# Written program order for three engines and the output weights' sums in a fused attention and SwiGLU layer

## The chip, the cores and the metric

The kernel runs on one core of a Trainium2 chip. The time is that of one execution of the whole program on the device, in microseconds (us); lower is better. A profile is one execution taken apart by the hardware profiler.

## What is computed

One layer (DEPTH = 1) with SEQ = 1024 rows, D_MODEL = 1024 and D_FF = 2816 in float32: attention with forget gates, then a SwiGLU feed-forward layer, each added to its input under a gate and normalised. The rest of the reference (the other mixer) isn't reached with one layer. What matters here is the second half of the loop body:

```python
def swiglu(h, w_in, w_out):
    gate, up = jnp.split(h @ w_in, 2, axis=-1)
    return (jax.nn.silu(gate) * up) @ w_out
...
        x = layer_norm(DEEPNORM_ALPHA * x + gate1 * y, ln_g[i, 0], ln_b[i, 0])
        h = x * (1.0 + scale2) + shift2
        x = layer_norm(DEEPNORM_ALPHA * x + gate2 * swiglu(h, ffn_w_in[i], ffn_w_out[i]), ln_g[i, 1], ln_b[i, 1])
```

## The kernel before

Each float32 operand is split into a high and a low part; a product takes three matmuls on TensorE (PE): high by high, high by low, low by high.

**The first feed-forward product** (h by the input weights) is where the change lies. It goes by hidden blocks of 128 columns, ff = 0 to 21, and multiplies 2 by 2 blocks with seven products in place of eight, called i = 1 to 7. Operand i of the weights is a part of the two weight tiles of the block (wi, gate half and up half) or a sum of such parts; operand i of h is a tile X or a part of h. The list `seq` holds the steps (ff, i): for the first six blocks products 1 and 2 alone are done first (12 steps, n = 0 to 11); then each of these blocks takes five steps (6, 7, 5, 4, 3), and each later block seven (1, 6, 2, 7, 5, 4, 3), 154 steps in all. `step(n)` does in this order:

- an eleventh of the output weights' sums, `out_weights(j, k)`, if one is due at this step (from step 42, ten steps for each j): loads of two weight tiles on the queue of SyncE (SP) at k = 0, two VectorE (DVE) subtractions at k = 7 (L1008, L1009), two more at k = 8 (L1011, L1012) and two stores of the result, the DRAM tile td, also on SP;
- the step's 12 matmuls (L1072 to L1074), which add into a PSUM bank: A for i = 1, 2; B for 6, 7, 4; D for 5, 3. Products of one bank accumulate, and between two of them the bank is read out;
- what is late: stores of hidden tiles, and for each pair of blocks four sums of hidden tiles, `hidden_sums`, on DVE (L990, L991, L994, L995);
- the read of the bank: i = 1 by a copy on ScalarE (ACT, L1081); i = 2 by ACT (L1083); i = 6 by DVE (L1085), which must be over before i = 7 adds into the same bank; i = 7 by DVE (L1087), before i = 4; i = 5 by DVE (L1089), before i = 3; i = 4 by DVE (L1092) and then GpSimd (POOL, L1093); i = 3 by DVE (L1096), ACT (L1097) and POOL (L1098);
- `prepare(n + 8)`: the weight operand of the step eight later goes into a ring of eight slots, the high part by ACT (L844), the low part by DVE (L845). At the first operand of a block, `sums(ff)` makes the sums: s1 for i = 5 (L828), s3 for i = 7 (L829), a21 in place for i = 6 (L830), s4 for i = 3 (L831), on DVE for ff < 2 and on POOL after that.

In the first steps the second half of the rows of h is still being made: `second_half(k)`, k = 0 to 3, and its later part `others`, transpose on PE, and make the five X tiles by ACT (L959, and L965 for the casts) and DVE (L960, L961, L966, L969, L970).

**The second product** (L1221 to L1223) follows, with a ring of its own: a cast by ACT (L1028) and a subtraction by DVE (L1029), and copies of PSUM by ACT (L1180).

**What sets the order.** The kernel is written as a sequence, but each engine's program is laid down by a scheduler, which moves an instruction ahead of others that it doesn't depend on, by its own estimate. Each engine then works its instructions off in that order.

Of the kernel before, what the change touches and what calls it, by code (L numbers as in the profile page):

```python
# [12 lines left out]
ALU = mybir.AluOpType  # L13
# [3 lines left out]
P = 128  # L17
# [22 lines left out]
def move(nc, dst, src):  # L40

    (nc.sync).dma_start(dst.bitcast(F32), src.bitcast(F32))


@with_exitstack
def fox_trunk_kernel(
# [17 lines left out]
    nc = tc.nc  # L64
# [5 lines left out]
    fwo = ffn_w_out[0]  # L70
# [230 lines left out]
    def qk_store(nm, ci, th):  # L301

        gi, dst = (0, qs) if nm[0] == "q" else (1, ks)
        g = gcol[:, gi:gi + 1]
        for p2 in range(2):
            st = bankS(f"st{nm}{th}{p2}")
            for i in range(4):
                qn = xh[nm, th * 4 + i].rearrange("p h d -> p (h d)")
                for k in range(2):
                    pr = p2 * 2 + k  # L310
                    nc.tensor.transpose(st[:, k, i * P:(i + 1) * P], qn[:, pr * P:(pr + 1) * P], ident)
            hi = pw.tile([P, 2, 512], F32R, name=f"qh{nm}{th}{p2}", tag="qth", bufs=1)
            lo = pw.tile([P, 2, 512], F32R, name=f"ql{nm}{th}{p2}", tag="qtl", bufs=1)
            nc.scalar.activation(hi, st, AF.Copy, scale=g)
            nc.vector.scalar_tensor_tensor(lo, st, g, f32(hi), op0=ALU.mult, op1=ALU.subtract)
            for k in range(2):
                d = dst[ci * 4 + p2 * 2 + k]
                for part, tl in ((0, hi), (1, lo)):
                    move(nc, d[part, :, th * 512:(th + 1) * 512], tl[:, k, :])

    def v_store(acc, tt, ci):
        vt = pv.tile([P, 4, 4, HD], F32R, name=f"vt{ci}{tt}", tag="vt", bufs=2)
        a4 = acc.rearrange("p (a b d) -> p a b d", b=2, d=HD)
        nc.scalar.copy(vt[:, :, 0::3, :], a4)
        nc.vector.tensor_tensor(vt[:, :, 1:3, :], a4, f32(vt[:, :, 0::3, :]), ALU.subtract)
        move(
            nc, vs[ci][:, tt * P:(tt + 1) * P, :].rearrange("h p e -> p h e"),
            vt.rearrange("p a b d -> p (a b d)").rearrange("p (h e) -> p h e", e=P),
        )

    def forget():
# [11 lines left out]
        def half(th):  # L343
# [40 lines left out]
            for r in range(2):  # L384
                move(nc, fq[:, r, cs], onesr)
                move(nc, fk[:, 2 + r, cs], onesr)
# [81 lines left out]
    def load(h):  # L468
        pr, s = divmod(h, 2)
        pool = ld[s]  # L470
        qa = pool.tile([P, T], F32R, name=f"qa{h}", tag="qa")
        ka = pool.tile([P, T], F32R, name=f"ka{h}", tag="ka")
        qb = pool.tile([68, T], F32R, name=f"qb{h}", tag="qb")
        kb = pool.tile([68, T], F32R, name=f"kb{h}", tag="kb")
        va = pool.tile([P, TT, P], F32R, name=f"va{h}", tag="va")
        rows = slice(s * HD, (s + 1) * HD)
        for r in range(2):
            move(nc, qa[r * HD:(r + 1) * HD, :], qs[pr][r, rows, :])
            move(nc, ka[r * HD:(r + 1) * HD, :], ks[pr][0, rows, :])
        move(nc, qb[0:HD, :], qs[pr][0, rows, :])  # L480
        move(nc, qb[HD:68, :], fq[h])
        move(nc, kb[0:HD, :], ks[pr][1, rows, :])
        move(nc, kb[HD:68, :], fk[h])
        move(nc, va, vs[h // 8][h % 8].rearrange("(k p) e -> p k e", p=P))
        return qa, qb, ka, kb, va
# [20 lines left out]
    first = load(0)  # L506
# [256 lines left out]
    def spill(tt):  # L763
        nc.sync.dma_start(x1d[tt], row(tt))
# [36 lines left out]
    def load_w(ff, n, tag):  # L801
        t = ld[0].tile([P, KT, P], F32, name=f"wi{ff}{n}_{len(opened)}", tag=tag, **({"bufs": 1} if tag == "owr" else {}))
        col = n * DFF + ff * P
        nc.sync.dma_start(t, fwi[:, col:col + P].rearrange("(k p) e -> p k e", p=P))
        opened.append(t)
        return t

    def load_raw(ff):
        raws[ff] = [load_w(ff, n, RAWS[ff % 2 * 2 + n]) for n in range(2)]
# [49 lines left out]
    td = [dram.tile([P, 2, 2, 512], F32, name=f"td{j}") for j in range(NJ)]  # L859
# [84 lines left out]
    def second_half(k):  # L944

        sp = bankS(f"h2t{k}")
        for n in range(2):
            for i in range(4):
                kt = n * 4 + k
                nc.tensor.transpose(sp[:, n, i * P:(i + 1) * P], row(HB * 4 + i)[:, kt * P:(kt + 1) * P], ident)  # L950
        a, a4 = [fp.tile([P, 512], F32, name=f"a{n}_{k}", tag=f"a{n}") for n in range(2)]
        for t, kt in ((a, k), (a4, k + 4)):
            nc.sync.dma_start(t, had[kt])
        hb = fp.tile([P, 512], F32, name=f"hb0_{k}", tag="hb0", bufs=2)
        ht = fp.tile([P, 2, 512], F32, name=f"ht_{k}", tag="hb1")
        hb4, t2 = ht[:, 0], ht[:, 1]
        for n, t in enumerate((hb, hb4)):
            kt = n * 4 + k
            nc.scalar.activation(t, sp[:, n, :], AF.Identity, scale=colA[:, kt:kt + 1], bias=colB[:, kt:kt + 1])  # L959
        nc.vector.tensor_tensor(a, hb, a, ALU.subtract)  # L960
        nc.vector.tensor_tensor(t2, hb4, a, ALU.subtract)  # L961

        def split(*parts):
            for n, t in parts:
                nc.scalar.copy(X[n][:, 0, k, :], t)  # L965
                nc.vector.tensor_tensor(X[n][:, 1, k, :], t, f32(X[n][:, 0, k, :]), ALU.subtract)  # L966

        def others():
            nc.vector.tensor_tensor(hb, hb4, hb, ALU.subtract)  # L969
            nc.vector.tensor_tensor(a4, a4, t2, ALU.subtract)  # L970
            split(("T3", hb), ("T4", a4), ("B22", hb4))
        split(("T2", t2), ("T1", a))
        return others

    banks, fds = {}, []

    def open_bank(tag, ff, n):
        banks[tag, ff] = psA.tile([P, 512], F32, name=f"{tag}{ff}", tag=tag, bufs=n)
# [21 lines left out]
    def out_weights(j, k):  # L1000

        b11, b12 = gate1b[:, 0:512], gate1b[:, 512:1024]
        b21, b22 = gate2b[:, 0:512], gate2b[:, 512:1024]
        if k == 0:
            for n, t in enumerate((gate1b, gate2b)):
                nc.sync.dma_start(t, fwo[(2 * j + n) * P:(2 * j + n + 1) * P, :])
        elif k == 7:
            nc.vector.tensor_tensor(b11, b12, b11, ALU.subtract)  # L1008
            nc.vector.tensor_tensor(b12, b22, b12, ALU.subtract)  # L1009
        elif k == 8:  # L1010
            nc.vector.tensor_tensor(b22, b22, b11, ALU.subtract)  # L1011
            nc.vector.tensor_tensor(b21, b21, b22, ALU.subtract)  # L1012
            for n, t in enumerate((gate1b, gate2b)):
                nc.sync.dma_start(td[j][:, n].rearrange("p c e -> p (c e)"), t)


    RING = 14
# [33 lines left out]
    def run_late(n):  # L1051

        for w in [w for w in late if w[0] <= n]:
            late.remove(w)
            w[1]()

    def step(n):
# [9 lines left out]
        if 0 <= j < NJ:  # L1067
            out_weights(j, k)
# [43 lines left out]
        prepare(n)  # L1112
    for ff in range(2):
        load_raw(ff)
    for n in range(n_first):
        step(n)
        if n in (3, 5, 7, 9):
            rest()
        if n in (2, 4, 6, 8):
            rest = second_half(n // 2 - 1)  # L1120
        if n == 8:
            for i in range(4):
                spill(HB * 4 + i)
    for n in range(n_first, len(seq)):
        step(n)
    run_late(len(seq) + 4)
    for cm in (fp_cm, psA_cm):
        cm.__exit__(None, None, None)
    fp = ctx.enter_context(tc.tile_pool(name="fo", bufs=1, side="right", reuse_waits="tile"))
# [173 lines left out]
```

## Time and profile before

| | |
|---|---|
| time, median of 3 runs | 1439.01 us (1437.71 to 1443.9) |
| profiled execution, its own time | 1438.14 us |
| its span, first to last instruction | 1436.3 us |
| mean granted clock of TensorE | 0.990 |
| busy: PE, DVE, ACT, POOL | 95%, 70%, 41%, 23% of the span |
| first feed-forward product | about 750 to 1211 us of the span |
| second product begins | about 1211 us |

Times in the rows are us from the start of the span. A timeline row has the start, the length, engine, line and operation; what stands in brackets is how long the engine had been idle and what ended that. The row of a window gives for each engine the busy time in it and, in brackets, its instructions.

### The profile page before, as it was taken

Reading aid. Unit: us, or ns where it says so; the run is one execution under the profiler, and the core shown is the slowest. Engines: PE = TensorE matmul, PEld = TensorE weight load, DVE = VectorE, ACT = ScalarE, POOL = GpSimd, SP = SyncE. Lnnn points to the kernel's source line nnn. Section 1 sums busy time; section 2 is a strip of 40 time slices with the busy share of each in tenths; the row PEclk is TensorE's granted clock in tenths of the full one; section 3 lists DMA queues with packets and bytes.
Section 4 is the critical chain, followed back from the end, with each engine's and each line's share of the span. In section 5 each row is a group of like instructions: output and inputs, shape, how many; then the busy total and the mean of one; then the engine's idle time right before and its main releaser. Section 6 shows DMA issues by size and latency. Waiting matters only on the chain.

```text
span 1436.3 us, 19137 instructions
## 1 busy us (share of the span) xinstructions
PE 1359.0 (95%) x6832; PEld 1134.0 (79%) x6832; DVE 1012.2 (70%) x1636; ACT 584.2 (41%) x1025; POOL 334.4 (23%) x250
## 2 busy tenths in 40 slices
PE   5899999999999999999999888999999999899997
PEld 4677778877888888879998667777788888788886
DVE  6866586555888888888778555767655556775897
ACT  3532232224777777774338222222223334533320
POOL 2442012210111111141000544434444431000011
PEclk9999999999999999999999999999999999999999
DMA  9757775558555555627463234777732336976531
GB/s 275 197 176 243 240 218 177 183 194 212 143 135 137 132 139 136 148 87 266 162 193 93 89 110 132 259 243 261 248 111 96 110 111 208 352 256 225 195 119 73
DMA packets 212305, 254.41 MB, mean 177 GB/s; under 512 B 13353, under 2 KB 138609, under 8 KB 212210
## 3 DMA queue, kind: packets, MB, share of 16 engines
q1 hardware_dynamic: 211058, 251.09, 57.9%
q10 hardware_dynamic: 1152, 2.10, 0.4%
q8 instruction: 54, 0.88, 0.3%
q14 instruction: 41, 0.34, 0.1%
HBM read 185.18 MB, written 67.96 MB: 176 GB/s over the span
## 4 chain that ended last, share of the span: by engine, by line
PE 63%; DVE 14%; DMA 9%; POOL 6%; issue 4%; ACT 2%; SPq 1%; POOLq 0%; DVEq 0%; ACTq 0%
PE og L631 5%; PE t L596 4%; PE y L1221 4%; PE y L1223 4%; PE y L1222 4%; PE B L1072 3%; PE B L1073 3%; PE B L1074 3%; PE s L535 2%; PE A L1072 2%; PE A L1074 2%; PE A L1073 2%; PE s L536 2%; PE o L579 2%; PE D L1074 2%
## 5 line engine op out<-in xcount | busy, mean ns | idle before, releaser
L1221 PE MATMUL y<-ring 128*128 128x512 f32 (+1 forms) x319 | 122.8, 385 | 4.7 <-ACT fpu L1180 4.3
L1072 PE MATMUL B<-XT,slots 128*128 128x512 f32 x264 | 106.9, 405 | 19.7 <-DVE fd L1085 16.7
L1029 DVE TENSOR_TENSOR ring<-r,ring 128x1024 fp32r<-128x1024 f32 x77 | 95.6, 1249 | 41.3 <-ACT ring L1028 36.2
L1028 ACT CAST ring<-r 128x1024 fp32r<-128x1024 f32 x77 | 80.5, 1053 | 107.7 <-PE y L1223 57.5
L1222 PE MATMUL y<-ring 128*128 128x512 f32 (+1 forms) x319 | 122.7, 385 | 0.0
L1223 PE MATMUL y<-ring 128*128 128x512 f32 (+1 forms) x319 | 122.4, 385 | 0.0
L602 DVE TENSOR_TENSOR pl<-t,ph 128x512 fp32r<-128x512 f32 x192 | 103.9, 549 | 14.8 <-ACT ph L601 13.4
L844 ACT CAST slots<-wi 128x512 fp32r<-128x512 f32 x88 | 54.2, 621 | 143.9 <-PE D L1073 73.0
L543 ACT ACTIVATE p<-s,nm 128x640 f32<-128x640 f32 (+7 forms) x128 | 95.5, 746 | 39.1 <-DVE nm L542 38.7
L601 ACT CAST ph<-t 128x512 fp32r<-128x512 f32 x192 | 90.9, 479 | 44.2 <-PE t L596 41.8
L1073 PE MATMUL B<-XT,slots 128*128 128x512 f32 x264 | 105.2, 399 | 0.0
L1074 PE MATMUL B<-XT,slots 128*128 128x512 f32 x264 | 105.0, 398 | 0.0
L542 DVE TENSOR_REDUCE nm<-s 128x1 f32<-128x640 f32 (+7 forms) x128 | 95.6, 748 | 2.5
L596 PE MATMUL t<-ident,p 128*128 128x128 f32 x576 | 95.7, 274 | 0.6 <-DVE pl L602 0.5
L596 PEld LDWEIGHTS t<-ident,p 128*128 128x128 f32 x576 | 71.3, 141 | 11.5 <-DVE pl L602 2.2
L1072 PEld LDWEIGHTS B<-XT,slots 128*128 128x128 f32 x264 | 50.9, 193 | 36.1 <-DVE fd L1085 21.8
L579 PE MATMUL o<-ph,va 128*128 128x512 f32 x192 | 76.6, 399 | 0.0
L845 DVE TENSOR_TENSOR slots<-wi,slots 128x512 fp32r<-128x512 f32 x88 | 71.0, 807 | 7.7 <-ACT slots L844 7.7
L1221 PEld LDWEIGHTS y<-ring 128*128 128x128 f32 x319 | 60.3, 189 | 18.1 <-ACT fpu L1180 4.7
L535 PE MATMUL s<-ka,qa 128*128 128x320 f32 (+2 forms) x192 | 67.5, 352 | 4.8 <-ACT p L543 4.8
L1223 PEld LDWEIGHTS y<-ring 128*128 128x128 f32 x319 | 60.4, 189 | 11.8
L1072 PE MATMUL A<-h2h,slots 128*128 128x512 f32 x176 | 69.2, 393 | 0.6 <-ACT fc L1081 0.6
(571 smaller groups left out, 3731.8 us busy)
## 6 DMA issues: line engine op xcount, KB each, us to landing
wi<-in_ffn_w_in_dram SPq DMA_DIRECT2D x50, 512.0 KB
aw<-in_ada_w_dram SPq DMA_DIRECT2D x46, 512.0 KB
r<-sd SPq DMA_DIRECT2D x77, 256.0 KB
sd<-hs SPq DMA_DIRECT2D x44, 256.0 KB
r<-td SPq DMA_DIRECT2D x44, 256.0 KB
sd<-fd SPq DMA_DIRECT2D x33, 256.0 KB
r<-in_ffn_w_out_dram SPq DMA_DIRECT2D x33, 256.0 KB
qa<-qs SPq DMA_DIRECT2D x32, 256.0 KB
```

The lines of the kernel that those rows point to most:

```text
L535: nc.tensor.matmul(o, qa[:, q], ka[:, c0:c0 + w], start=True, stop=False)
L542: nc.vector.tensor_reduce(nm, view, axis=axis, op=ALU.max, negate=True)
L579: nc.tensor.matmul(o[:, c0:], va[:, kbk, :], ph[:, c0:], start=(kbk == 0), stop=False)
L596: nc.tensor.transpose(tb[:, jj * P:(jj + 1) * P], probs[hf * 4 + jj][:, kbk * P:(kbk + 1) * P], ident)
L602: nc.vector.tensor_tensor(pl[:, c0:], tb[:, c0:], f32(ph[:, c0:]), ALU.subtract)
L1029: nc.vector.tensor_tensor(t[:, 1], raw, f32(t[:, 0]), ALU.subtract)
L1072: nc.tensor.matmul(b, hi, rh, start=(first and k == 0), stop=False, skip_group_check=True)
L1073: nc.tensor.matmul(b, hi, rl, start=False, stop=False, skip_group_check=True)
L1074: nc.tensor.matmul(b, lo, rh, start=False, stop=(k == 3), skip_group_check=True)
L1221: nc.tensor.matmul(b[:, c0:c1], sh, wh, start=first, stop=False, skip_group_check=True)
L1222: nc.tensor.matmul(b[:, c0:c1], sh, wl, start=False, stop=False, skip_group_check=True)
L1223: nc.tensor.matmul(b[:, c0:c1], sl, wh, start=False, stop=last, skip_group_check=True)
```

## The change

A new function, `written_order`, goes over the instructions in the order in which the kernel's text issued them and binds each one of ACT, DVE and POOL to the one before it on the same engine, with a dependence that the scheduler must keep but that puts no semaphore on the chip. It is called after the last step of the first product, for what was issued since the first step. PE and SP are not in its list. In `out_weights`, `tc.keep_in_program_order` is put around the loads, the four subtractions and the stores. No instruction is added or taken away.

```diff
+def written_order(tc, first, engines):
+
+    last = {}
+    for ins in tc.nc.cur_bb.bb.instructions[first:]:
+        if ins.engine not in engines:
+            continue
+        if ins.engine in last:
+            tc.add_manual_dep(ins, last[ins.engine],
+                              mybir.DependencyInfo(mybir.DependencyClass.NoSync, mybir.DependencyReason.DATA),
+                              reason="written order")
+        last[ins.engine] = ins.name
...
+    keep = tc.keep_in_program_order
...
         if k == 0:
             for n, t in enumerate((gate1b, gate2b)):
-                nc.sync.dma_start(t, fwo[(2 * j + n) * P:(2 * j + n + 1) * P, :])
+                keep(nc.sync.dma_start(t, fwo[(2 * j + n) * P:(2 * j + n + 1) * P, :]))
         elif k == 7:
-            nc.vector.tensor_tensor(b11, b12, b11, ALU.subtract)
-            nc.vector.tensor_tensor(b12, b22, b12, ALU.subtract)
+            keep(nc.vector.tensor_tensor(b11, b12, b11, ALU.subtract))
+            keep(nc.vector.tensor_tensor(b12, b22, b12, ALU.subtract))
         elif k == 8:
...
+    traced = len(nc.cur_bb.bb.instructions)
     for n in range(n_first):
         step(n)
...
     run_late(len(seq) + 4)
+    written_order(tc, traced, (mybir.EngineType.Activation, mybir.EngineType.DVE, mybir.EngineType.Pool))
```

The subtractions at k = 8 and the stores of td are wrapped in the same way. New lines shift the line numbers of the changed kernel: sums L828 to L831 become L841 to L844, L844 and L845 become L857 and L858, L990, L994, L995 become L1004, L1008, L1009, the output weights' L1008, L1009, L1011, L1012 become L1022, L1023, L1025, L1026, and the reads L1081, L1085, L1087, L1089, L1092, L1093, L1096, L1097, L1098 become L1095, L1099, L1101, L1103, L1106, L1107, L1110, L1111, L1112.

**GpSimd, the sums of block 14.** The wi140 and wi141 tiles are the gate and the up half of block 14. Before, from the row behind the last sum of block 13 on (the first L1093 and L1098 are those of block 11, the last two those of block 12):

```order
L1093 TENSOR_TENSOR fd_8631<-fd_8631,fc_8277 128x512
L1098 TENSOR_TENSOR fd_8631<-fd_8631 128x512
L829 TENSOR_TENSOR sqb_8409<-wi140_35_9958,wi141_36_9960 128x512
L828 TENSOR_TENSOR sqb_8409<-wi141_36_9960 128x512
L830 TENSOR_TENSOR wi141_36_9960<-sqb_8409,wi140_35_9958 128x512
L831 TENSOR_TENSOR skb_8410<-wi140_35_9958,wi141_36_9960 128x512
L1093 TENSOR_TENSOR fd_8631<-fd_8631,fc_8277 128x512
L1098 TENSOR_TENSOR fd_8631<-fd_8631 128x512
```

Of the change, from L1112 of block 12 on (L1107 and L1112 further down are those of block 13):

```order
L1112 TENSOR_TENSOR fd_8631<-fd_8631 128x512
L841 TENSOR_TENSOR sqb_8409<-wi141_36_9960 128x512
L842 TENSOR_TENSOR sqb_8409<-wi140_35_9958,wi141_36_9960 128x512
L843 TENSOR_TENSOR wi141_36_9960<-sqb_8409,wi140_35_9958 128x512
L844 TENSOR_TENSOR skb_8410<-wi140_35_9958,wi141_36_9960 128x512
L1107 TENSOR_TENSOR fd_8631<-fd_8631,fc_8277 128x512
L1112 TENSOR_TENSOR fd_8631<-fd_8631 128x512
L841 TENSOR_TENSOR sqb_8409<-wi151_38_10095 128x512
```

The four sums of a block now stand behind the last GpSimd operation of the block two before it, where they stood one block earlier, and L828 is now ahead of L829.

**VectorE, the first five-step blocks.** B1 is the bank of block 1, hs3_1 a hidden sum of blocks 0 and 1. Before:

```order
L1096 TENSOR_TENSOR fd_8631<-D0_8666,fd_8631 128x512
L845 TENSOR_TENSOR slots_7830<-sqb_8409,slots_7830 128x512
L994 TENSOR_TENSOR hs3_1_8840<-fd_8631 128x512
L1085 TENSOR_TENSOR fd_8631<-B1_8719,fc_8277 128x512
L845 TENSOR_TENSOR slots_7830<-wi21_12_8543,slots_7830 128x512
```

Of the change, at the same read of bank B1 (L1099 is L1085):

```order
L1106 TENSOR_TENSOR fd_8631<-B0_8630,fc_8277 128x512
L858 TENSOR_TENSOR slots_7830<-sqb_8409,slots_7830 128x512
L1110 TENSOR_TENSOR fd_8631<-D0_8666,fd_8631 128x512
L858 TENSOR_TENSOR slots_7830<-sqb_8409,slots_7830 128x512
L1099 TENSOR_TENSOR fd_8631<-B1_8719,fc_8277 128x512
L858 TENSOR_TENSOR slots_7830<-wi21_12_8543,slots_7830 128x512
L1101 TENSOR_TENSOR fd_8631<-B1_8719,fc_8277 128x512
L858 TENSOR_TENSOR slots_7830<-skb_8410,slots_7830 128x512
```

The hidden sum L994 stood ahead of the read of bank B; it is now behind it.

**VectorE, the second half of h, k = 1.** XT2_8272, XT1_8274, XT3_8273, XT4_8275 and XB22_8276 are the X tiles for i = 6, 5, 7, 4 and 3, hb0_1 and ht_1 what ACT makes of the transposes (L959). Before:

```order
L960 TENSOR_TENSOR a0_1_8426<-hb0_1_8430,a0_1_8426 128x512
L845 TENSOR_TENSOR slots_7830<-sqb_8409,slots_7830 128x512
L961 TENSOR_TENSOR ht_1_8431<-ht_1_8431,a0_1_8426 128x512
L966 TENSOR_TENSOR XT1_8274<-a0_1_8426,XT1_8274 128x512
L969 TENSOR_TENSOR hb0_1_8430<-ht_1_8431,hb0_1_8430 128x512
L966 TENSOR_TENSOR XT2_8272<-ht_1_8431,XT2_8272 128x512
L970 TENSOR_TENSOR a1_1_8427<-a1_1_8427,ht_1_8431 128x512
L966 TENSOR_TENSOR XT3_8273<-hb0_1_8430,XT3_8273 128x512
L966 TENSOR_TENSOR XB22_8276<-ht_1_8431,XB22_8276 128x512
L966 TENSOR_TENSOR XT4_8275<-a1_1_8427,XT4_8275 128x512
```

Of the change (L973, L974, L982, L983 and L979 are L960, L961, L969, L970 and L966):

```order
L973 TENSOR_TENSOR a0_1_8426<-hb0_1_8430,a0_1_8426 128x512
L974 TENSOR_TENSOR ht_1_8431<-ht_1_8431,a0_1_8426 128x512
L979 TENSOR_TENSOR XT2_8272<-ht_1_8431,XT2_8272 128x512
L979 TENSOR_TENSOR XT1_8274<-a0_1_8426,XT1_8274 128x512
L858 TENSOR_TENSOR slots_7830<-sqb_8409,slots_7830 128x512
L982 TENSOR_TENSOR hb0_1_8430<-ht_1_8431,hb0_1_8430 128x512
L983 TENSOR_TENSOR a1_1_8427<-a1_1_8427,ht_1_8431 128x512
L979 TENSOR_TENSOR XT3_8273<-hb0_1_8430,XT3_8273 128x512
L979 TENSOR_TENSOR XT4_8275<-a1_1_8427,XT4_8275 128x512
L979 TENSOR_TENSOR XB22_8276<-ht_1_8431,XB22_8276 128x512
L858 TENSOR_TENSOR slots_7830<-sqb_8409,slots_7830 128x512
```

The low parts now come in the order in which the text has them, T2 and T1 first, and no operation of `others` stands between L960 and the low part of T1 any more.

The subtractions of the output weights stand at their written steps in the changed program; in blocks 7 and 17 L1011 and L1012 (as L1025 and L1026), in block 14 L1008 and L1009, come between the low part of the next block's i = 6 (L845) and the read of bank B (L1085). On SP the loads and stores of the output weights, which all stood in the first half of the blocks, are now spread over the steps up to the last block, and the last store of td stands near the first loads of the second product's ring. In the second product ACT's first copies L1180 come after the cast of r2_18, where they came after that of r2_22.

## Rows read from the trace of the kernel before

**Rows 1.** The page, section 1: busy us, share of the span, instructions.
```profile
PE   1359.0 (95%) x6832; PEld 1134.0 (79%) x6832; DVE 1012.2 (70%) x1636; ACT 584.2 (41%) x1025; POOL 334.4 (23%) x250
```

**Rows 2.** Stretches: window, its us, busy per engine (instructions), granted clock, DMA share, GB/s.
```profile
800.00:900.00 100.00, 87.79 (x355) 70.42 (x354) 52.90 (x69) 22.34 (x36) 44.46 (x32) 0.93 0.35 113
900.00:1000.00 100.00, 93.33 (x397) 74.84 (x396) 72.31 (x99) 27.02 (x46) 41.98 (x29) 0.98 0.75 256
...
1100.00:1200.00 100.00, 100.00 (x443) 82.87 (x442) 50.15 (x74) 31.32 (x52) 36.61 (x26) 1.00 0.35 116
1200.00:1300.00 100.00, 95.33 (x412) 77.95 (x411) 76.61 (x69) 47.82 (x50) 3.69 (x2) 0.98 0.87 294
```

**Rows 3.** TensorE's waits from 806 to 890 us: total us, times, longest.
```profile
PE B L1072 <- DVE fd L1085: 12.2, 5, 2.7
```

**Rows 4.** TensorE's waits from 890 to 1215 us.
```profile
PE D L1072 <- DVE fd L1089: 5.5, 3, 2.3
PE B L1072 <- DVE fd L1085: 3.2, 5, 1.0
PE A L1072 <- ACT fc L1081: 0.6, 1, 0.6
```

**Rows 5.** Timeline around 811 us (start, length, engine; idle before, releaser).
```profile
807.32 1.28 POOL L1098 TENSOR_TENSOR fd<-fd 128x512 f32<-128x512 f32 x1
...
808.63 1.73 DVE L994 TENSOR_TENSOR hs<-fd 128x512 f32<-128x512 f32 x1 [2.64 <-POOL fd L1098]
...
810.29 0.68 DVE L1085 TENSOR_TENSOR fd<-B,fc 128x512 f32<-128x512 f32 x1
...
811.02 0.80 PE L1072 MATMUL B<-XT,slots 128*128 128x512 f32 x1 [2.73 <-DVE fd L1085]
...
815.66 0.69 DVE L1087 TENSOR_TENSOR fd<-B,fc 128x512 f32<-128x512 f32 x1 [3.61 <-PE B L1074]
```

**Rows 6.** Timeline of one undisturbed block (block 18 and the end of 17).
```profile
1134.59 0.39 PE L1072 MATMUL A<-h2h,slots 128*128 128x512 f32 x1
...
1142.75 0.39 PE L1072 MATMUL B<-XT,slots 128*128 128x512 f32 x1
...
1136.23 1.29 POOL L1098 TENSOR_TENSOR fd<-fd 128x512 f32<-128x512 f32 x1 [1.72 <-ACT fd L1097]
...
1147.04 1.28 POOL L828 TENSOR_TENSOR sqb<-wi 128x512 f32<-128x512 f32 x1 [1.55 <-DVE slots L845]
...
1149.77 1.62 POOL L831 TENSOR_TENSOR skb<-wi,wi 128x512 f32<-128x512 f32 x1
...
1149.00 1.24 DVE L845 TENSOR_TENSOR slots<-wi,slots 128x512 fp32r<-128x512 f32 x1
```

**Rows 7.** Timeline around 796 us: a sum, and TensorE after it.
```profile
794.86 1.28 POOL L830 TENSOR_TENSOR wi<-sqb,wi 128x512 f32<-128x512 f32 x1
...
798.69 0.50 PE L1072 MATMUL B<-XT,slots 128*128 128x512 f32 x1 [3.06 <-DVE fd L1087]
```

**Rows 8.** Timeline of the second half's transposes, 766 to 783 us.
```profile
768.99 0.69 DVE L960 TENSOR_TENSOR a<-hb,a 128x512 f32<-128x512 f32 x1
...
782.24 0.69 DVE L960 TENSOR_TENSOR a<-hb,a 128x512 f32<-128x512 f32 x1
...
766.18 0.62 ACT L965 CAST XT<-a 128x512 fp32r<-128x512 f32 x1
...
766.70 0.78 ACT L959 ACTIVATE hb<-h2t,colB,colA 128x512 f32<-128x512 f32 x1
```

**Rows 9.** Timeline at the start of the second product.
```profile
1244.22 0.56 PE L1221 MATMUL y<-ring 128*128 128x512 f32 x1 [4.32 <-ACT fpu L1180]
...
1238.73 1.05 ACT L1028 CAST ring<-r 128x1024 fp32r<-128x1024 f32 x1 [0.33 <-DMA r<-td]
...
1242.64 1.04 ACT L1028 CAST ring<-r 128x1024 fp32r<-128x1024 f32 x1 [0.30 <-DMA r<-td]
```

**Rows 10.** Timeline: a sum of the output weights beside GpSimd's work.
```profile
908.64 1.80 DVE L1008 TENSOR_TENSOR gate1b<-gate1b 128x512 f32<-128x512 f32 x1 [2.85 <-DMA gate1b<-in_ffn_w_out_dram]
```

More of the change, by code (lines that the diff above doesn't have):

```diff
@@ L1005, in out_weights @@
             for n, t in enumerate((gate1b, gate2b)):
-                nc.sync.dma_start(t, fwo[(2 * j + n) * P:(2 * j + n + 1) * P, :])
+                keep(nc.sync.dma_start(t, fwo[(2 * j + n) * P:(2 * j + n + 1) * P, :]))
         elif k == 7:
-            nc.vector.tensor_tensor(b11, b12, b11, ALU.subtract)
-            nc.vector.tensor_tensor(b12, b22, b12, ALU.subtract)
+            keep(nc.vector.tensor_tensor(b11, b12, b11, ALU.subtract))
+            keep(nc.vector.tensor_tensor(b12, b22, b12, ALU.subtract))
         elif k == 8:
-            nc.vector.tensor_tensor(b22, b22, b11, ALU.subtract)
-            nc.vector.tensor_tensor(b21, b21, b22, ALU.subtract)
+            keep(nc.vector.tensor_tensor(b22, b22, b11, ALU.subtract))
+            keep(nc.vector.tensor_tensor(b21, b21, b22, ALU.subtract))
             for n, t in enumerate((gate1b, gate2b)):
-                nc.sync.dma_start(td[j][:, n].rearrange("p c e -> p (c e)"), t)
+                keep(nc.sync.dma_start(td[j][:, n].rearrange("p c e -> p (c e)"), t))
     RING = 14
```

## The prediction

> **What bounds the kernel now.** I read the page's busy times first: PE works 95% of the span [rows 1], so a change of order can only give back PE's idle time, or add to it. The stretches of 100 us show where that idle time is [rows 2]: between 800 and 900 us PE is busy for 87.79 us at a granted clock of 0.93, between 900 and 1000 for 93.33, and between 1100 and 1200 for 100.00 at full clock. The first product thus starts badly and ends perfectly. PE's waits name what it lacks: in the five-step blocks 1 to 5 the read of bank B, L1085, five times, 12.2 us in all [rows 3]; in the seven-step blocks 9.3 us, in nine waits [rows 4], all before 1040 us, while the output weights are being summed.
>
> The timeline at 811 us shows how the first kind comes about [rows 5]. L1085 needs nothing but the bank, but L994, a hidden sum, stands ahead of it on DVE and waits for POOL's L1098, which ends at 808.60. L994 then takes 1.73 us, L1085 can start at 810.29, and PE at 811.02. PE also comes back slowly: the step's read L1087 starts 4.64 us after PE's start, where the same distance in an undisturbed block is 2.92 (12 matmuls of 0.227 and about 0.2 to the read).
>
> **The change, term by term.** No instruction comes or goes; only positions change. All sums are made against the profiled execution, 1438.14 us, 0.87 below the median of the three runs.
>
> *A, the start (block 0).* Before, DVE runs the second half of h without a gap: from the first operation L960 of one part to that of the part two later 13.25 us pass [rows 8], 6.62 each, or 11 operations at 0.60. In the new order the low part of T2 comes straight behind L961 and must wait for ACT's cast of T2 (0.62), and the next L960 waits for ACT's L959 (0.78), which stands in turn behind the last cast of the part before, a read of a bank and a weight cast, 0.62 or so each. Each part so gains two gaps of DVE, of 0.7 and of 0.7 to 1.5 us: 8.0 to 8.8 us for 6.62. Over four parts that is +5.6 to +8.7 at DVE. The present wait of 3.06 us for L1087 [rows 7] came from sums of block 2 that ACT had ahead of it, and those come later now, so some is covered. **I take +6.4**, ends +3 and +9.
>
> *B, blocks 1 to 5.* L994 and L990 now stand behind L1085. The 12.2 us go [rows 3], except what the read itself costs between i = 6 and i = 7, some 0.5 us a block, and two places where hidden sums delay another read by one operation, 0.7 each: +3.9 at most, I take +3.4. The clock comes back too: the step above lost 4.64 − 2.92 = 1.7 us; three such losses make 5.1, and the window's clock of 0.93 allows 7.0 [rows 2]. I take 5.5. **B = −12.2 + 3.4 − 5.5 = −14.3**, ends −11 and −18.
>
> *C, blocks 6 to 20.* This is the term that decides. Before, the sums of block ff + 1 were made long ahead, for they stood one block earlier on POOL. Now they stand behind L1098 of block ff − 1, and on both ACT and DVE the cast and the low part of operand i = 6 of block ff + 1, which need L830, stand ahead of the read L1085 of block ff. So PE can't go on to i = 7 before this chain is over, counted in an undisturbed block [rows 6]:
> – i = 1 starts on PE at 1134.59; L1098 of the block before ends at 1137.52, i.e. 2.93 after it;
> – L828, L829, L830 follow, 1.28 to 1.29 each and 0.08 between (L828 to L831 with one operation in between): 3 × 1.37 = 4.11, so to 1141.63;
> – then cast, low part, read and PE. The same four links stand once in the trace: L830 ended at 796.14 and PE started at 798.69 [rows 7], 2.55 us. So PE starts i = 7 at 1144.18.
> It was due at 1142.75, three steps after i = 1. **The wait is 1.43 us in each of 15 blocks.** The POOL operation that meets a low part of DVE takes 1.62 rather than 1.29 [rows 6], one of the chain does: +0.33. The first matmul after a wait takes 0.50 for 0.39: +0.1. That makes 1.86, or 27.9 in all. In blocks 7 and 17 two sums of the output weights stand inside the chain, in block 14 two as well, in four or so more blocks one meets a POOL operation; a sum takes 0.69 alone and 1.80 at worst [rows 10]: I take +5, ends 0 and +11. What goes: the nine waits, 9.3 us, with their slow first matmuls (0.9) and the clock lost between 900 and 1000 us (2%, some 1.6): −11.8. **C = 27.9 + 5 − 11.8 = +21**, ends +10 (15 × 1.43 alone) and +28.
>
> [...]
>
> *New clock losses.* In the old stretch from 900 to 1000 us, with waits of up to 2.3 us, the clock still was 0.98. Waits of 1.5 to 2 should mostly leave it alone; the start and three or four blocks with longer ones may lose 1 to 1.7 each. **+4**, ends 0 and +9.
>
> *D, the second product's start.* PE waits 4.32 us at 1244.22 for ACT's copies L1180 [rows 9], which stand behind the cast of r2_22 (1242.64). Behind that of r2_18 (1238.73) they run 3.9 us earlier. The wait nearly goes, and the clock lost with it (0.98 over 100 us, some 1.7). Against that, the last stores of td, 1 MB, now fall next to the ring's first loads, where the DMA engines are busy at 0.87 [rows 2]. **D = −4**, ends 0 and −6.
>
> *The queues.* SP's loads and stores of the output weights move to their written steps; each load must wait for the stores two steps before it (5.4 us), and has seven steps (19 us) until L1008. I cost this at nothing; its cover is that slack.
>
> Sum: 6.4 − 14.3 + 21 + 4 − 4 = **+13**, so 1438.1 + 13 = **1451 us**.
>
> **The rivals.**
>
> 1. *Faster: the sums chain does not bind.* C turns on one comparison: from the end of i = 3 to PE's i = 7 the chain has three steps, 8.16 us, and I have 9.59 for it. If ACT and POOL run it in under 8.16, the wait is nil and only what goes is left: 6.4 − 14.3 − 11.8 − 4 = −24, so **1414**. For it: 9.59 is built from one undisturbed block and one tail of a disturbed one. Against it: all four GpSimd operations would have to be 0.36 shorter than any that I see. Chance 0.08.
> 2. *About the same: the chain binds at its least.* 15 × 1.43 = 21.5, no meetings, no clock lost, A at its low end: 3 − 14.3 + 21.5 − 11.8 − 4 = −6 to, with A at 6.4 and meetings at half, +3: **1433 to 1443**. Chance 0.20.
> 3. *Much slower: the regular waits pull the clock down.* PE would now pause in every block, some 20.9 us apart. If each of 15 waits costs the 1.7 us seen at 811 us, that adds 21 to C in place of the 4: **1468**. For it: rows 5; against it: nine waits between 890 and 1040 us went with a clock of 0.98. [...] A load of output weights that comes late, with reads queued behind L1008 (2.85 us once, rows 10), would end in the same place: 7 blocks × 2.85 = +20. Chance for both 0.17.
>
> That the change doesn't do what it says is excluded by the program order.
>
> **How the numbers follow.** My forecast, 1444 to 1460, has 0.55; the rivals have the rest. The range reaches from the middle of rival 2 to the lower part of rival 3: **1437 to 1466**; the unknown terms (A ±3, meetings +6/−5, clock +5/−4, D +4/−2) give about the same. Half a per cent, 7.2 us around 1439.0, is what a measurement of this kernel can tell from no change. Slower than 1446.2: most of the forecast's 0.55 (0.50) and 0.17, **0.67**. Same: **0.25**. Faster: rival 1, **0.08**.
>
> **What would show it.** Right: the windows between 1100 and 1200 us no longer show PE at 100.00 but near 92; PE's waits have some 15 of 1.5 to 2 us on L1085 in blocks 6 to 20, each behind a low part that waited for ACT and ACT for L830; the waits of 2.73 in blocks 1 to 5 are gone and that stretch's clock is near 1.0; block 0's i = 4 starts about 805 us rather than 798.69. Wrong: no waits in 1100 to 1200 (rival 1); a clock under 0.95 there (rival 3); reads behind a sum of the output weights that waits for DMA.

## The result and the profile after

The change makes the kernel slower: 1459.94 us (median of 4 runs, 1455.35 to 1461.77) against 1438.36 for the kernel before in the same comparison; the ratio of the means is 1.0137, 95% interval 1.0102 to 1.0172. The forecast was 1451 in a range of 1437 to 1466.

The waits of TensorE (PE) in the same stretches as [rows 3, 4], the second one taken to 1245 us since the product ends later:

```profile
PE B L1086 <- DVE fd L1099: 1.7, 5, 0.3
PE B L1086 <- ACT slots L857: 1.1, 2, 0.6
PE B L1086 <- DVE fd L1101: 0.8, 1, 0.8
```

```profile
PE B L1086 <- DVE fd L1099: 32.2, 15, 3.6
```

The 12.2 us of waits for bank B's read in blocks 1 to 5 are down to 1.7 (the 0.8 for L1101 is still block 0's), and the nine waits of 9.3 us that came after have been replaced by one wait in every block from 6 to 20, all for the same read of bank B, L1099. The stretches, columns as in [rows 2], with PE's busy us first and the granted clock third from the end:

```profile
800.00:900.00 100.00, 93.86 (x390) 73.96 (x391) 62.08 (x78) 24.61 (x42) 53.10 (x36) 0.97 0.37 118
900.00:1000.00 100.00, 90.28 (x380) 72.86 (x379) 58.15 (x76) 25.40 (x44) 37.78 (x26) 0.97 0.48 161
...
1100.00:1200.00 100.00, 91.92 (x390) 74.36 (x389) 58.13 (x78) 26.01 (x45) 38.45 (x27) 0.97 0.47 156
```

From 1100 to 1200 us, where PE had been busy for 100.00, it now is for 91.92 at a clock of 0.97. The profile's page gives PE 94% of the span:

```profile
PE 1369.9 (94%) x6832; PEld 1137.2 (78%) x6832; DVE 1024.1 (70%) x1636; ACT 581.0 (40%) x1025; POOL 340.0 (23%) x250
```

That is 10.9 us more of PE's busy time than in [rows 1] for the same instructions. Over the whole span, then, half of the loss is not idle time but matmuls that take longer; the mean granted clock of the span is 0.985 for 0.990.

To divide the loss I use the DVE reads of the i = 3 products of blocks 0, 5 and 20. Before:

```profile
804.48 0.69 DVE L1096 TENSOR_TENSOR fd<-D,fd 128x512 f32<-128x512 f32 x1 [1.43 <-PE D L1074]
...
892.29 0.69 DVE L1096 TENSOR_TENSOR fd<-D,fd 128x512 f32<-128x512 f32 x1 [0.33 <-PE D L1074]
...
1191.91 0.69 DVE L1096 TENSOR_TENSOR fd<-D,fd 128x512 f32<-128x512 f32 x1 [1.43 <-PE D L1074]
```

After:

```profile
813.03 0.69 DVE L1110 TENSOR_TENSOR fd<-D,fd 128x512 f32<-128x512 f32 x1 [1.43 <-PE D L1088]
...
886.31 0.69 DVE L1110 TENSOR_TENSOR fd<-D,fd 128x512 f32<-128x512 f32 x1 [1.43 <-PE D L1088]
...
1219.31 0.69 DVE L1110 TENSOR_TENSOR fd<-D,fd 128x512 f32<-128x512 f32 x1 [1.43 <-PE D L1088]
```

| stage | before | after | difference |
|---|---|---|---|
| up to block 0 | 804.5 | 813.0 | +8.5 |
| blocks 1 to 5 | 87.8 | 73.3 | −14.5 |
| blocks 6 to 20 | 299.6 | 333.0 | +33.4 |
| from there to the end of the span (1436.3, 1458.4) | 244.4 | 239.1 | −5.3 |
| sum | | | +22.1 |

The start loses 8.5 us, blocks 1 to 5 and the end gain more than that; what makes the kernel slower is blocks 6 to 20, which lose 33 us. An undisturbed seven-step block takes 19.04 us (seven steps of 2.72, a third of the 8.16 between PE's two starts in [rows 6]), 15 of them 285.6. So before, blocks 6 to 20 lost 14.0 us, and after, 47.4.

**One block of the 15.** The timeline of block 16, POOL first, then ACT, DVE and PE:

```profile
1108.52 1.29 POOL L1112 TENSOR_TENSOR fd<-fd 128x512 f32<-128x512 f32 x1 [1.72 <-ACT fd L1111]
1109.78 1.74 POOL L841 TENSOR_TENSOR sqb<-wi 128x512 f32<-128x512 f32 x1
1111.47 1.29 POOL L842 TENSOR_TENSOR sqb<-wi,wi 128x512 f32<-128x512 f32 x1
1112.84 1.30 POOL L843 TENSOR_TENSOR wi<-sqb,wi 128x512 f32<-128x512 f32 x1
1114.22 1.28 POOL L844 TENSOR_TENSOR skb<-wi,wi 128x512 f32<-128x512 f32 x1
```

```profile
1114.17 1.15 ACT L857 CAST slots<-wi 128x512 fp32r<-128x512 f32 x2 [3.78 <-POOL wi L843]
```

```profile
1107.09 0.69 DVE L1110 TENSOR_TENSOR fd<-D,fd 128x512 f32<-128x512 f32 x1 [1.43 <-PE D L1088]
...
1114.83 1.23 DVE L858 TENSOR_TENSOR slots<-wi,slots 128x512 fp32r<-128x512 f32 x1 [4.46 <-ACT slots L857]
1115.98 0.68 DVE L1099 TENSOR_TENSOR fd<-B,fc 128x512 f32<-128x512 f32 x1
```

```profile
1116.71 0.50 PE L1086 MATMUL B<-XT,slots 128*128 128x512 f32 x1 [1.50 <-DVE fd L1099]
```

This is the forecast chain, link by link. L1112 of block 15 ends at 1109.81, the three sums of block 17 up to L843 at 1114.14, ACT's cast L857 starts 0.03 later, the low part L858 at 1114.83, the read L1099 at 1115.98, and PE at 1116.71: 2.57 us from L843's end, where [rows 7] gave 2.55. L841 takes 1.74, where L842 takes 1.29: a low part of DVE (L858, 1108.99 to 1110.36) runs beside it. PE's wait is shown as 1.50, since a matmul's own time (0.39) runs 0.16 past the next one's start (0.23 apart); counted from start to start, and with the slower first matmul, such a block takes 20.84 us, 1.80 above 19.04.

### The profile page after: what moved, and what is told of

It is laid out like the page before. It is cut to its first block, busy times and chain, and to the rows that moved or that the text cites. A ratio compares the mean times of both kernels' runs of the same rounds, so it can differ in the third digit from the quotient of the medians.

```text
span 1458.4 us, 19129 instructions
## 1 busy us (share of the span) xinstructions
PE 1369.9 (94%) x6832; PEld 1137.2 (78%) x6832; DVE 1024.1 (70%) x1636; ACT 581.0 (40%) x1025; POOL 340.0 (23%) x250
## 4 chain that ended last, share of the span: by engine, by line
PE 58%; DVE 14%; POOL 9%; DMA 6%; ACT 6%; issue 5%; SPq 1%; POOLq 0%; DVEq 0%; ACTq 0%
PE og L644 5%; PE y L1237 4%; PE y L1238 4%; PE y L1239 4%; PE t L609 4%; PE B L1086 3%; PE B L1087 3%; PE B L1088 3%; PE D L1087 2%; PE D L1088 2%; PE D L1086 2%; PE s L548 2%; PE s L549 2%; PE o L592 2%; PE o L593 2%
## 5 line engine op out<-in xcount | busy, mean ns | idle before, releaser
L1086 PE MATMUL B<-XT,slots 128*128 128x512 f32 x264 | 111.7, 423 | 42.3 <-DVE fd L1099 39.6
L858 DVE TENSOR_TENSOR slots<-wi,slots 128x512 fp32r<-128x512 f32 x88 | 82.7, 940 | 83.4 <-ACT slots L857 83.4
L1043 DVE TENSOR_TENSOR ring<-r,ring 128x1024 fp32r<-128x1024 f32 x77 | 92.6, 1223 | 33.3 <-ACT ring L1042 31.5
L1087 PE MATMUL B<-XT,slots 128*128 128x512 f32 x264 | 107.9, 409 | 0.2 <-DVE XT L979 0.2
L1088 PE MATMUL B<-XT,slots 128*128 128x512 f32 x264 | 107.4, 407 | 0.0
L857 ACT CAST slots<-wi 128x512 fp32r<-128x512 f32 x88 | 52.6, 618 | 116.3 <-POOL wi L843 62.4
L1107 POOL TENSOR_TENSOR fd<-fd,fc 128x512 f32<-128x512 f32 x20 | 32.8, 1641 | 203.2 <-DVE fd L1106 203.2
L1237 PEld LDWEIGHTS y<-ring 128*128 128x128 f32 x319 | 60.0, 188 | 14.3 <-ACT fpu L1196 1.7
```

Of the source, the lines that this page charges most:

```text
L1086: nc.tensor.matmul(b, hi, rh, start=(first and k == 0), stop=False, skip_group_check=True)
L1087: nc.tensor.matmul(b, hi, rl, start=False, stop=False, skip_group_check=True)
L1088: nc.tensor.matmul(b, lo, rh, start=False, stop=(k == 3), skip_group_check=True)
L1237: nc.tensor.matmul(b[:, c0:c1], sh, wh, start=first, stop=False, skip_group_check=True)
```

## Experiments

Line numbers below are those of the changed kernel.

**GpSimd left out of the order.** Only POOL's program differs from the change.

```diff
-    written_order(tc, traced, (mybir.EngineType.Activation, mybir.EngineType.DVE, mybir.EngineType.Pool))
+    written_order(tc, traced, (mybir.EngineType.Activation, mybir.EngineType.DVE))
```

> GpSimd left out of the written order; its sums go back to where they stood before, one block earlier, and no instruction of ScalarE, VectorE, SyncE or TensorE moves. Theory (the sums behind L1112 end the chain): the 15 waits for L1099 in blocks 6 to 20, 32.2 us, fall under 4, the clock of 900 to 1200 us returns to 0.99 or more, blocks 6 to 20 go from 333 to 288-292 us, the time to 1410-1420 us. Rival 1 (the written order of ScalarE and VectorE itself, operand ahead of the read, makes the wait): the 1.50 us stay in each block, 1455-1462 us. Rival 2 (the pauses of the start carry most of it): below 10 us gained, 1448-1456.

1417.11 us, ratio to the kernel before 0.983 (0.9801 to 0.9859). Stretch and waits of blocks 6 to 20:

```profile
885.00:1175.00 290.00, 287.53 (x1264) 236.32 (x1263) 202.00 (x252) 87.36 (x150) 127.77 (x87) 1.00 0.55 182
```

```profile
PE B L1086 <- DVE fd L1101: 1.2, 2, 0.6
PE D L1086 <- DVE fd L1103: 1.0, 2, 0.5
PE A L1086 <- ACT fc L1095: 0.3, 1, 0.3
```

The block-20 read comes 289.6 us after that of block 5, not 333.0, and no wait for L1099 is left, only 2.5 us for other reads. The place of the sums on POOL accounts for 43 of the 47 us. Rival 1 falls with the waits; the start is as late as in the change (812.7), so rival 2 falls too.

**The same by the text.** All three engines ordered, but the sums called two steps earlier.

```diff
         if n + 8 < len(seq):
             prepare(n + 8)
+            if ff >= 5 and i == 5 and ff + 2 < NF:
+                left[ff + 2] = sums(ff + 2)
```

> All three engines keep the written order, but the text itself calls the sums of block ff + 2 at the end of step (ff, 5), two steps earlier, for ff from 5 on. Theory: as with GpSimd free, 1410-1420 us, no wait for L1099 over 0.5 us in blocks 6 to 20. Rival 1 (the operand ahead of the read is what waits): 1455-1462. Rival 3 (the sums then delay L1107 and L1112, and these the silu and the stores that free a bank): new waits on banks B or D of about 1 us a block, 1425-1440.

1415.17 us, ratio 0.9816 (0.9786 to 0.9845). Blocks 6 to 20 take 287.8 us. So it is not the written order as such that costs, but one place in it.

**One more operation in the chain.**

```diff
-        eng.tensor_tensor(s1, a21, a22, ALU.add)
+        for _ in range(1 + (ff > 6)):
+            eng.tensor_tensor(s1, a21, a22, ALU.add)
```

> The changed kernel with the first sum of each block from ff = 7 on made twice on GpSimd, so one operation of 1.29 us more (1.37 with the gap) stands in the chain; nothing is left out. Theory (the sums on GpSimd end the chain in every block): each of the 15 waits for L1099 grows by 1.37, from 1.50 to 2.87 where it is least and 32.2 to about 53 us in all; 1479-1482 us from the waits alone, up to 1500 if waits of 2.9 us pull the clock down where those of 1.5 did not. Rival (GpSimd has slack and another engine ends the chain): below 1464 us, waits unchanged.

1497.54 us, ratio 1.038 (1.0341 to 1.042). The read of bank B is L1100 here:

```profile
PE B L1087 <- DVE fd L1100: 52.1, 15, 4.9
```

```profile
900.00:1200.00 300.00, 258.04 (x1029) 207.17 (x1028) 156.88 (x211) 69.33 (x121) 118.30 (x84) 0.91 0.43 141
```

The least wait is 2.83, so 1.33 more, and the sum 52.1 where 53 was expected: POOL has no slack in this chain. But blocks 6 to 20 became 35.3 us longer (368.3 between the reads of blocks 5 and 20), and only 19.9 of that are waits. The rest goes with the clock: 0.91 over 300 us, where the change had 0.97.

**Keeping the output weights' work alone.** The call of `written_order` is left out.

> Only the output weights' loads, subtractions and stores keep their place; no written order for the three engines. Theory: the start and blocks 1 to 5 as in the kernel before (804.5 and 892 us at the third-product reads of blocks 0 and 5), the sums where they stood before; of the 9.3 us of waits in blocks 6 to 20 some half stays, the second product's wait of 4.3 us falls to 1-2; 1430-1437 us. Rival (the spread of these loads and sums over all blocks is what costs): 15 or so waits in blocks 6 to 20 and 1450 us or more.

1422.96 us, ratio 0.9856 (0.982 to 0.9892), below the expected range. Blocks 1 to 5 stay slow (86.9 us), as expected. Blocks 6 to 20, between the reads at 892.33 and 1177.96:

```profile
892.00:1178.00 286.00, 286.00 (x1264) 236.78 (x1263) 180.57 (x252) 89.44 (x150) 126.55 (x87) 1.00 0.55 184
```

PE is busy without a gap; not half but all of the 14.0 us that the kernel before loses there is gone. So those were made by the place of the output weights' work, and spreading it is a gain of its own. This run doesn't tell the loads from the subtractions; the run with both edits but without keeping (below) clears the same stretch with only the subtractions tied, by DVE's order. The second product's first wait stayed (4.77 us), against my expectation.

**Order without keeping.** `keep` becomes a function that returns its argument.

> Written order for the three engines, but the loads and stores of the output weights are not kept; up to the end of the first product only some loads and stores on SyncE's queue move, and in the second product the first copies L1196 of ScalarE come after the cast of r2_22 again. Theory: the first product as in the change (1.50 us in each of 15 blocks), and the second product's first wait 2-4 us longer: 1460-1465 us. Rival (that place of L1196 is worth nothing, since the loads end the wait): 1457-1461, with the same wait of about 1.3 us.

1461.8 us, ratio 1.0142 (1.0102 to 1.0181). The first product has the same 15 waits (32.1 us); the second product's first wait:

```profile
PE y L1237 <- ACT fpu L1196: 4.9, 1, 4.9
```

It is 4.9 rather than 1.3. The copies L1196 stand only one cast later than in the change, not four as I had taken it to be. That cast, with its load, accounts for some 1.35 us, my estimate from the distance of two such casts in the change (1265.59 to 1266.94). The casts ahead of it also come later: the low part behind the first of the last group (L1043) starts at 1268.34 for 1262.83, 5.5 us, where PE's end of the first product moved by 3.2. In the change L1164 stands before these casts on ACT, after 8.94 us of idle time for the load of ln_g. The profiled execution took 1468.84 us, the other three 1461.14 to 1462.06, so whether those waited as long isn't shown.

**VectorE alone.** `written_order` with DVE only.

> Written order for VectorE alone; ScalarE and GpSimd are laid down by the scheduler. Against the run with GpSimd free only ScalarE's order differs. Theory (the gain of blocks 1 to 5 is VectorE's order, the loss at the start VectorE and ScalarE waiting in turn): blocks 1 to 5 take 73 us as in the change, block 0's third-product read comes at 806-813 us, blocks 6 to 20 as with GpSimd free: 1408-1418 us. Rival (ScalarE's order carries the gain of blocks 1 to 5): these take 80-88 us and the time is 1425-1435.

1412.13 us, ratio 0.9788 (0.9759 to 0.9817). Block 0's read at 813.5, blocks 1 to 5 in 71.2 us, 6 to 20 in 287.7. DVE's order carries both the gain of blocks 1 to 5 and the loss at the start; adding ACT's order to it, as in the run with GpSimd free, changes neither by more than 2 us.

**Order from step 12 on.**

```diff
-    traced = len(nc.cur_bb.bb.instructions)
     for n in range(n_first):
...
+    traced = len(nc.cur_bb.bb.instructions)
     for n in range(n_first, len(seq)):
```

> The written order binds only from step 12 on; the second half of h is laid down by the scheduler again. Theory (the start's ping-pong of ScalarE and VectorE costs 8.5 us at the end of block 0): the 5.68 us wait of block 0 falls to about 1.2, the third-product read of block 0 comes at 801-805 in place of 813.0 us, all later blocks as in the change; 1446-1453 us. Rival (block 0 is late through what follows, sums of blocks 1 and 2 on GpSimd): unchanged, 1457-1462.

1452.26 us, ratio 1.0073 (1.0051 to 1.0095). Block 0's read:

```profile
803.18 0.69 DVE L1110 TENSOR_TENSOR fd<-D,fd 128x512 f32<-128x512 f32 x1 [1.43 <-PE D L1088]
```

It comes 9.9 us earlier, and the time is 7.7 us lower (the kernel before took 2.9 us longer in this comparison than in the first one); the rest of the first product is as in the change (73.3 and 331.8 us).

**Both edits** (sums earlier, order from step 12).

> Sums two steps earlier in the text and the written order only from step 12 on. Theory: both gains add up, 1400-1410 us, about 30 us under the kernel before. Rival (the two share a wait, or the gained stretch is lost at the second product, whose loads then come later than TensorE): 1415-1430.

1406.58 us, ratio 0.9749 (0.9715 to 0.9783). The gains add up: 1459.94 less 7.7 (order from step 12) and 44.8 (sums earlier) would be 1407.4.

**Both edits without keeping.**

> The run with both edits (sums earlier, order from step 12), but without keeping the output weights' loads and stores. In the first product no engine but SyncE's queue moves; in the second the copies L1196 come after r2_22's cast again. Theory: first product the same (third-product read of block 20 at 1160.9 us within 1.5), a wait of some 4-5 us at the second product's start in place of 0.6, with its clock: 1410-1413 us. Rival (keeping place is what cleared blocks 6 to 20): waits of about 9 us come back there, 1416-1422.

1407.58 us, ratio 0.9788 (0.9754 to 0.9822). The first product is the same (block 20's read at 1161.0); the second product's first wait is 2.6 us rather than 0.6, half of what I expected. In time the two can't be told apart.

**VectorE alone, from step 12 on.**

> Written order for VectorE alone, and only from step 12 on, with the output weights' work kept in place; ScalarE and GpSimd are laid down by the scheduler. Theory: the gain of blocks 1 to 5 and of the kept sums without the loss at the start or in blocks 6 to 20: 1400-1407 us, the same as or a little under the run with both edits (1406.6). Rival (without ScalarE's order the start still loses, since VectorE's order alone made block 0 end at 813.5 us): 1410-1414.

1402.35 us, ratio 0.9741 (0.9719 to 0.9762): the best of all, though its interval overlaps that of both edits. The reads of blocks 0, 5 and 20:

```profile
802.57 0.69 DVE L1110 TENSOR_TENSOR fd<-D,fd 128x512 f32<-128x512 f32 x1 [1.43 <-PE D L1088]
...
873.43 0.69 DVE L1110 TENSOR_TENSOR fd<-D,fd 128x512 f32<-128x512 f32 x1 [0.97 <-PE D L1088]
...
1161.11 0.69 DVE L1110 TENSOR_TENSOR fd<-D,fd 128x512 f32<-128x512 f32 x1 [1.43 <-PE D L1088]
```

It has the early start (802.6), the fast blocks 1 to 5 (70.9) and the undisturbed blocks 6 to 20 (287.7).

## Why the prediction was right

The direction, the place and the mechanism held; the time lies 9 us above the forecast, in the upper half of the range, since some terms were too small. Two sums among the rivals don't come out as printed: the upper end of rival 2 is 1441 by its own terms, not 1443, and that of rival 3 is about 1473, not 1468 (15 × 1.7 = 25.5 in place of the 4). Neither changes the forecast.

*A, the start.* +8.5 for +6.4. The timeline of DVE has the operation L973 (L960 before) of three parts in turn, and between them the low part of T2 (L979) and the ring's low parts (L858) with their waits for ACT:

```profile
771.46 0.69 DVE L973 TENSOR_TENSOR a<-hb,a 128x512 f32<-128x512 f32 x1
...
773.63 0.69 DVE L979 TENSOR_TENSOR XT<-ht,XT 128x512 fp32r<-128x512 f32 x1 [0.68 <-ACT XT L978]
...
775.16 0.69 DVE L858 TENSOR_TENSOR slots<-sqb,slots 128x512 fp32r<-128x512 f32 x1 [0.23 <-ACT slots L857]
...
779.27 0.69 DVE L858 TENSOR_TENSOR slots<-sqb,slots 128x512 fp32r<-128x512 f32 x1 [0.22 <-ACT slots L857]
779.95 0.69 DVE L973 TENSOR_TENSOR a<-hb,a 128x512 f32<-128x512 f32 x1
...
788.44 0.69 DVE L973 TENSOR_TENSOR a<-hb,a 128x512 f32<-128x512 f32 x1
```

L973 to L973 is 8.49 us, inside the 8.0 to 8.8 of the working, where [rows 8] gave 6.62. The first gap is the forecast one (0.68); the second is not one gap but several of 0.2 or so. Block 0's read of bank B so comes 8.4 us late (800.25 for 791.87), within the +5.6 to +8.7 of the working. From there the vanished wait of 3.06 us should have given something back. Before, in block 0:

```profile
792.62 0.50 PE L1072 MATMUL B<-XT,slots 128*128 128x512 f32 x1 [1.20 <-DVE fd L1085]
```

After, with a window of the same place:

```profile
800.99 0.80 PE L1086 MATMUL B<-XT,slots 128*128 128x512 f32 x1 [5.68 <-DVE fd L1099]
...
807.26 0.51 PE L1086 MATMUL B<-XT,slots 128*128 128x512 f32 x1 [0.79 <-DVE fd L1101]
```

```profile
801.00:807.00 6.00, 5.47 (x12) 3.79 (x12) 1.71 (x2) 0.92 (x2) 4.91 (x4) 0.50 0.30 87
```

The wait for L1101 did fall to 0.79. But PE had waited for 5.68 us just before, and the granted clock here is 0.50: from i = 7 to i = 4 it takes 6.27 us, where the kernel before took 6.07 (792.62 to 798.69 [rows 7]). In the run with both edits without keeping, whose order also begins at step 12 and whose wait there is 1.22, the same step took 3.80 (790.42 to 794.22). What the working missed is thus the clock: it allowed the start 1 to 1.7 us, and it cost some 2.5. That DVE's order alone makes the start late was shown by the run with DVE only.

*B, blocks 1 to 5.* −14.5 for −14.3, and the parts hold too: the waits fell from 12.2 to 2.9 us, −9.3 for the −8.8 of the working, and the rest, −5.2 for −5.5, goes mostly with the clock, 0.92 over this stage before and 1.00 after. The 0.5 us a block that the working took for the read itself stood on no row; in the change PE's waits for it are 1.7 us over five, 0.3 each.

*C, blocks 6 to 20.* This is where the 9 us lie. The least wait was right: 15 × 1.80 = 27.0 for 27.9. Three parts were too small, two costs and one gain:
– the extras: 32.2 us of waits less 15 × 1.50 leave 9.7, for +5. Blocks 7 and 17 wait 3.58, 10 and 20 3.14, 14 2.83, 13 2.39, so six blocks are longer where the working had seven or so, but each by more. In block 14 two subtractions stand before the read (+1.33). In block 13 L1112 comes 0.9 us late, because two subtractions stood ahead of the read L1110; in 10 and 20 this adds to a stretch of the sums (0.74). In block 7 two things add: L1025 and L1026 stand between the operand and the read, as foreseen, but L1022 and L1023 also run beside POOL's sums and stretch L842 and L843 to 1.74 and 1.62. I had counted the stretch of DVE's operations and not that of POOL's, which lies in the chain:

```profile
909.84 1.74 POOL L841 TENSOR_TENSOR sqb<-wi 128x512 f32<-128x512 f32 x1
911.53 1.74 POOL L842 TENSOR_TENSOR sqb<-wi,wi 128x512 f32<-128x512 f32 x1
913.35 1.62 POOL L843 TENSOR_TENSOR wi<-sqb,wi 128x512 f32<-128x512 f32 x1
```

```profile
910.35 1.78 DVE L1022 TENSOR_TENSOR gate1b<-gate1b 128x512 f32<-128x512 f32 x1
912.16 1.66 DVE L1023 TENSOR_TENSOR gate1b<-gate2b,gate1b 128x512 f32<-128x512 f32 x1
915.65 1.21 DVE L858 TENSOR_TENSOR slots<-wi,slots 128x512 fp32r<-128x512 f32 x1 [1.83 <-ACT slots L857]
916.79 0.68 DVE L1025 TENSOR_TENSOR gate2b<-gate2b,gate1b 128x512 f32<-128x512 f32 x1
917.50 0.69 DVE L1026 TENSOR_TENSOR gate2b<-gate2b 128x512 f32<-128x512 f32 x1
918.11 0.68 DVE L1099 TENSOR_TENSOR fd<-B,fc 128x512 f32<-128x512 f32 x1
```

– the clock: 333.0 − 285.6 − 27.0 − 9.7 = 10.7 us, for +4 (of which some was meant for the start). In the trace each of the six waits of 2.39 us or more is followed by a stretch of 3.3 to 5.5 us in which a matmul takes 0.63 instead of 0.39 us; after none of the nine waits of 1.50 is there one. The example of block 7, where PE had waited until 918.85, with the window of the slow stretch (clock 0.50) and one behind block 16's wait of 1.50 (clock 1.00):

```profile
918.85 0.50 PE L1086 MATMUL B<-XT,slots 128*128 128x512 f32 x1 [3.58 <-DVE fd L1099]
...
919.91 0.63 PE L1087 MATMUL B<-XT,slots 128*128 128x512 f32 x1
```

```profile
920.00:923.00 3.00, 3.00 (x9) 2.32 (x8) 0.00 (x0) 0.00 (x0) 0.00 (x0) 0.50 0.95 264
1116.80:1120.00 3.20, 3.20 (x14) 2.65 (x15) 3.17 (x6) 0.41 (x1) 0.00 (x0) 1.00 0.33 87
```

– what goes: 14.0 us for 11.8. The run that only keeps the output weights' work shows it whole.
So 27.0 + 9.7 + 10.7 − 14.0 = +33.4.

*D, the second product.* −5.3 for −4: its first wait fell from 4.32 [rows 9] to 1.29 us, and no slow stretch follows it.

```profile
1268.52 0.50 PE L1237 MATMUL y<-ring 128*128 128x512 f32 x1 [1.29 <-ACT fpu L1196]
```

Counted in the traces, 23 casts of the ring stood ahead of the first copy before, and 19 in the change. (The cast at 1238.73, which the prediction names r2_18, is the 21st in the trace before; the 19th started at 1236.01.) In the eight traces with 19 casts ahead the wait is 0.6 to 1.9 us, in the two with 20 it is 2.6 (both edits without keeping) and 4.9 (order without keeping), with 21 it is 4.8 (keeping alone). With 23, before, it was 4.32. More casts ahead go with a longer wait, but the price of one cast isn't shown apart from that of the loads.

*The queues* cost nothing: no read in blocks 6 to 20 stood behind a sum that waited for a load.

*The rivals.* Rival 1 was priced at 1414 for the case that the chain doesn't bind; the run with GpSimd free, which makes that case, took 1417. Rival 3 came in part: the clock in 900 to 1200 us is 0.97, not under 0.95. In the run with one more operation it is 0.91, and there it does what the rival says: of the 82.7 us above 285.6, 56.6 are the waits with their slow restart, and 26 are left for the clock, 1.7 a block. A slow stretch followed all six waits of 2.39 us or more in the change, 13 of 15 waits of 2.83 or more in the run with one more operation, and three of the five waits of 2.73 to 3.06 us in blocks 0 to 4 of the kernel before. So no length of wait here decides it alone. The 1.50 us of nine blocks in the change, which recur as regularly, cost nothing of the kind.

*DVE beside POOL.* In the lines of block 7, L841 ends at 911.58 and L1022 at 912.13, 0.55 later; L842, begun meanwhile at 911.53, ends 1.14 after L1022; L1023 ends 0.55 after L842, and L843 1.15 after L1023. So it is wherever the two overlap between 800 and 1215 us of the changed kernel's trace: 59 DVE operations with two SBUF inputs, begun beside one running GpSimd operation, end 0.53 to 0.60 us after it, whatever the overlap, and 54 GpSimd operations begun beside such a DVE operation end 1.13 to 1.16 after that. The 11 bank reads beside a GpSimd operation, which have one input in PSUM and one in SBUF, kept their 0.68 or 0.69. The low part in [rows 6] fits as well (L830 ends at 1149.69, the low part 0.55 later), and so does L858 in block 16, which ends 0.56 after L844. C's tail of 2.55 us, from [rows 7], already holds such a low part, begun beside L831 (at 796.83, 1.21 us, its end 0.55 after L831's).

## What to carry to other kernels

A written order is worth as much as the place of each step in it: before fixing it, go through the text for steps whose result is needed by an instruction that stands in front of something urgent, here the three sums between L1112 and the read of a bank, and call them earlier. Compare the chain with the time that the bottleneck engine gives it (9.6 us against three steps of 2.72), and look for operations of VectorE that run beside a GpSimd operation of the chain, or the other way round: in the change such operations took up to 1.78 us for 0.69 on VectorE and up to 1.75 for 1.29 on GpSimd. A change with several parts is worth taking apart: here a gain of 14 and one of 14.5 us were hidden under one loss of 47.

## What was not expected of the hardware

The cost of a wait on PE was not proportional to it. In the run with one more GpSimd operation, 19.9 us more waiting made blocks 6 to 20 longer by 35.3 us, while the granted clock over 900 to 1200 us fell from 0.97 to 0.91, and the slow matmuls (0.63 for 0.39 us) came in 13 stretches over the 15 blocks rather than in 6. And a DVE operation with two SBUF inputs beside a GpSimd one went with a longer time of both: L1022 took 1.78 for 0.69 us and L842 beside it 1.74 for 1.29.
